# Splitting attention keys once and copying the other half by DMA, value weights' low parts on VectorE, roots one tile later

## The chip, the cores and the metric

The kernel runs on one core of one Trainium2 chip. A core has five engines, each with its own instruction queue: TensorE (PE in the profile, with its weight loads as PEld), VectorE (DVE), ScalarE (ACT), GpSimd (POOL) and the sync engine (SP), which issues all of this kernel's DMAs. Each queue is worked off in order; an instruction that waits holds back what stands behind it on its engine. Tensors lie on chip in 128 partitions. The metric is the device time of one launch in microseconds (us), as the median of several runs; one more launch was profiled.

## The reference, cut to what matters

The reference is two layers of a diffusion backbone over 512 latent tokens and 256 context tokens, 1024 wide, in float32. The change lies in layer 0, grouped-query attention with 16 query heads and 4 key and value heads of 64 elements:

```
q_l, k_l, v_l = split(h_lat @ w_qkv)
q_l = rope(rms_norm(q_l, q_norm));  k_l = rope(rms_norm(k_l, k_norm))
k_c, v_c likewise for the context, normed, without rope
s = einsum(q, k) * HEAD_DIM ** -0.5
o = einsum(softmax(s), v) @ w_o
```

Latent queries attend to all 768 keys, context queries to the 256 context keys. Behind it come a gated feed-forward layer with a short convolution, a Mamba-2 layer in both directions and a second feed-forward layer. All of these take most of the time and are not edited.

## The kernel before, in words

Activations are kept transposed: features on partitions, tokens in columns (512 latent, then 256 context). To keep float32 accuracy every operand of the large products is split into a high part, rounded to TensorE's reduced float32, and a low part, what the rounding left; a product then takes three matmuls: high by high, high by low and low by high (`mm3`, L105 to L108). `split` (L81) does this with a cast on ScalarE (L85) and a subtraction on VectorE or GpSimd (L87).

Attention starts with a stage written out by hand, in which PE multiplies the latent tokens by six column tiles of the query and key weights into `ps_l`. The loop that the change edits comes next (L694 to L705). For the same six tiles, in the order 0, 1, 2, 4, 5, 3, it multiplies the context tokens (24 matmuls into `ps_c`) and copies the result behind the latent columns of `raw0` to `raw5`. Tile 0 holds keys 0 and 1 (two heads of 64 elements, one on each half of the partitions), tile 1 the first two query heads, tile 3 keys 2 and 3, the others more queries.

Between the tiles stand steps of two generators, `keys(0, ...)` and `queries(0, ...)`. Both begin with `normed` (L526): squares (L529) and gain (L530) on ScalarE, a copy of the latent columns with neighbouring groups of 32 partitions swapped by four DMAs (`qsw`, L533), the rotary turn in three VectorE operations (L534 to L536), sums over each head by matmuls with two columns (`ssq`, L236), the inverse root (`rsa`, `rsy`, `rsu`, `rbq`, L239 to L247), a transposition of the root by PE (`rsTq`, L253, four and then two blocks of 128 tokens), and the multiplication by it (L540). `normed` yields after `rbq`, and after each of the two groups of transpositions. So the step in which PE transposes needs the `rbq` of the step before. `keys` then makes, for each of its two heads, a high and a low tile in which the head stands on both halves of the partitions (L547 to L555), since two query heads, one per half, are multiplied by the same key head; `queries` splits into `qh` and `ql`.

Also in this loop the two halves of the value weights are loaded and split (`wv`), the low parts on GpSimd (`wl`). When the loop is done, 48 steps of `values` (three matmuls each into `ps_v`, L521) are walked through; at every fifth a step of `pairs[0].maxima()` stands between them (L602: scores of the high parts only, whose row maxima on VectorE, L604, give the shift `diag` of the softmax), and at every sixth a step of the queries of pair 1. Then follow eight pairs of query heads with scores (`ps_s`, L674), exponentials (`pr`, L677) and products with the values (`ps_o`, L638); pair p uses key head p // 2. Keys 2 and 3 are made during these pairs (`keys(1, ...)`), with the rotary turn on GpSimd.

A scheduler sets the order behind the hand-written stage: it takes the instructions by the order in which the program wrote them and by a model of when each can start. Tiles of 128x768 come from a ring of 18 buffers (`t3`).

Of the kernel before, what the change touches and what calls it, by code (L numbers as in the profile page):

```python
# [9 lines left out]
F32R = mybir.dt.float32r  # L10
AF = mybir.ActivationFunctionType
ALU = mybir.AluOpType
# [55 lines left out]
def t3(g, name, dt=F32, n=T):  # L68
    return g.t3p.tile([P, n], dt, tag="t3", bufs=g.n3, name=name)
# [6 lines left out]
def _r(ap):  # L76

    return ap.bitcast(F32)


def split(g, src, hi, lo, lo_engine="dve", pin=False):  # L81

    nc = g.nc
    keep = g.tc.keep_in_program_order if pin else lambda i: i
    keep(nc.scalar.copy(hi, src))  # L85
    eng = nc.vector if lo_engine == "dve" else nc.gpsimd
    keep(eng.tensor_tensor(lo, src, _r(hi), ALU.subtract))  # L87


def load_w(g, dram, lo_engine="dve", pin=False):  # L90

    st = t4(g, "wst")
    wh = t4(g, "wh", F32R)
    wl = t4(g, "wl", F32R)
    g.nc.sync.dma_start(st, dram)
    split(g, st, wh, wl, lo_engine=lo_engine, pin=pin)
    return wh, wl
# [282 lines left out]
def attention(g, fill, X, late):  # L380


    nc, I = g.nc, g.I
    S64 = slice(0, 64), slice(64, 128)
# [62 lines left out]
    e = g.p.tile([P, 2 * KT], F32, name="silu")  # L447
# [8 lines left out]
    rsl, _, _ = next(norm)  # L456
# [12 lines left out]
    for m in range(KT):  # L469
# [14 lines left out]
        if m == 4:  # L484
            rsc = t3(g, "rsc", n=C)
            pt, _, _ = next(norm)
# [23 lines left out]
    wv = []  # L510
# [33 lines left out]

    def keys(j, qs, eng):
        yield from normed(qs, kn, eng)
        for e in range(2):  # L547

            h, l = t3(g, f"kh{j}{e}", F32R), t3(g, f"kl{j}{e}", F32R)
            s, o = S64[e], S64[1 - e]  # L550
            nc.scalar.copy(h[s], qs[s])
            nc.scalar.copy(h[o], qs[s])
            nc.vector.tensor_tensor(l[s], qs[s], _r(h)[s], ALU.subtract)
            nc.scalar.copy(l[o], _r(l)[s])
            k2[2 * j + e] = (h, l)  # L555
        yield 0

    qprep = {}
# [26 lines left out]
    class Pair:  # L585
# [6 lines left out]
        def maxima(self):  # L592


            qh, kh = qprep[self.p][0], k2[self.kv][0]
            lat, ctx, mz = small("ma"), small("mb"), small("mz")

            def scores(ts, k0, n, out):
                ps = Sb("ps_m")
                for i, t in enumerate(ts):  # L600
                    for e in range(2):
                        nc.tensor.matmul(ps[:, 512 * e + n * i : 512 * e + n * i + n], qh[S64[e], t * P : (t + 1) * P],  # L602
                                         kh[S64[e], k0 : k0 + n], start=True, stop=True)
                nc.vector.reduce_max(out[:, :, ts[0] : ts[-1] + 1], ps.rearrange("p (e t k) -> p e t k", e=2, k=n),  # L604
                                     axis=AX.X, negate=True)

            scores((4, 5), L, C, lat)
            nc.vector.tensor_copy(ctx[:, :, 4:], lat[:, :, 4:])
            yield
            for t in (0, 2):  # L610
                scores((t,), 0, L, lat)
                yield
                scores((t + 1,), 0, L, lat)
                yield
                scores((t, t + 1), L, C, ctx)
                if t:

                    for e in range(2):
                        for h in range(2):
                            nc.vector.tensor_tensor(mz.rearrange("p h t -> p t h")[S64[e], :, h], lat[S64[h], e],  # L620
                                                    ctx[S64[h], e], ALU.min)
                    self.diag = g.t3p.tile([P, T], F32R, tag="mrow", bufs=2, name=f"diag{self.p}")
                    v = self.diag.rearrange("p (t h q) -> p t h q", h=2, q=64)
                    for h in range(2):
                        nc.vector.tensor_tensor(v[:, :, h], id2.unsqueeze(1).broadcast_to([P, T // P, 64]),
                                                mz[:, h].unsqueeze(2).broadcast_to([P, T // P, 64]), ALU.mult)
                yield

        def steps(self):

            (qh, ql), (kh, kl) = qprep[self.p], k2[self.kv]
            po = acc = None
            o = g.t3p.tile([P, T], F32, tag="o", bufs=2, name=f"o{self.p}")

            def values(po, pr, t, off, n, first, last):
                v = vt[t][:, self.kv * HD : (self.kv + 1) * HD]
                for e in range(2):
                    nc.tensor.matmul(po[S64[e], :n], v, pr[:, 512 * e + off : 512 * e + off + n], start=first, stop=last)  # L638

            def final(po, ps, acc, out):  # L640

                n = out.shape[-1]
                for e in range(2):
                    nc.tensor.matmul(ps[S64[e], :n], g.ones[:, :HD], acc[:, n * e : n * e + n], start=True, stop=True)
                y, u = t2("y")[:, :n], t2("u")[:, :n]

                nc.scalar.activation(y, ps, AF.Ln)
                nc.scalar.activation(y, y, AF.Exp, scale=-1.0)
                nc.vector.tensor_tensor(out, po, y, ALU.mult)
                nc.vector.scalar_tensor_tensor(u, ps, -1.0, y, ALU.mult, ALU.mult)  # L650
                nc.vector.scalar_tensor_tensor(out, u, 2.0, out, ALU.add, ALU.mult)

            def later_lat(po, pr, t, acc):
                values(po, pr, t, 0, L, t == 0, t == 5)
                if t == 5:
                    final(po, Bk("ps_sum"), acc, o[:, :L])

            def later_ctx(pr, acc):
                pc = Bk("ps_oc")
                for t in range(2):  # L660
                    values(pc, pr, 4 + t, C * t, C, t == 0, t == 1)
                final(pc[:, :C], pc[:, C:], acc, o[:, L:])
                if self.p < 6:
                    nc.sync.dma_start(odram[self.p], o)

            prev = None
            for t in range(7):
                ps, pr = Sb("ps_s"), g.t3p.tile([P, 1024], F32, tag="pr", bufs=3, name="pr")
                for q0, n, k0, off in (((0, L, t * P, 0),) if t < 6 else ((L, C, L, 0), (L, C, L + P, C))):
                    q, k = slice(q0, q0 + n), slice(k0, k0 + P)  # L670
                    outs = [ps[:, 512 * e + off : 512 * e + off + n] for e in range(2)]
                    for i, (a, b) in enumerate(((kh, qh), (kl, qh), (kh, ql))):
                        for e in range(2):
                            nc.tensor.matmul(outs[e], a[S64[e], k], b[S64[e], q], start=i == 0, stop=False)  # L674
                    for e in range(2):
                        nc.tensor.matmul(outs[e], onesr[S64[e]], self.diag[S64[e], q], start=False, stop=True)  # L676
                nc.scalar.activation(pr, ps, AF.Exp)  # L677
                if t == 0:
                    po = Bk("ps_o")
                elif t == 1:  # L680
                    acc = g.t3p.tile([P, 1024], F32, tag="acc", bufs=1, name="acc")
                    nc.vector.tensor_tensor(acc, prev, pr, ALU.add)
                elif t < 6:
                    nc.vector.tensor_tensor(acc, acc, pr, ALU.add)
                else:
                    acc = t2("accc")
                    halves = pr.rearrange("p (e k q) -> p e k q", e=2, k=2)
                    nc.vector.tensor_tensor(acc.rearrange("p (e q) -> p e q", e=2), halves[:, :, 0], halves[:, :, 1], ALU.add)
                prev = pr
                yield (lambda t=t, pr=pr, po=po, acc=acc: later_lat(po, pr, t, acc)) if t < 6 else (  # L690
                    lambda pr=pr, acc=acc: later_ctx(pr, acc))
            g.o.append(o)

    early = []  # L694
    for n, j in enumerate((0, 1, 2, 4, 5, 3)):
        ps = Bk("ps_c")
        for k in range(KT):
            k_step(k, j, ps[:, :C], hc)
        nc.scalar.copy(raw[j][:, L:], ps[:, :C])
        if n in (1, 3):  # L700
            wv.append(load_w(g, I["wv"][len(wv)], lo_engine="pool", pin=True))
        if n in (1, 2):
            early.append(keys(0, raw[0], nc.vector) if n == 1 else queries(0, raw[1], nc.vector))
        for gen in early:
            next(gen, None)  # L705
    vals = values()
    for gen in early:
        for _ in gen:
# [22 lines left out]

    m = pairs[0].maxima()
    for i, _ in enumerate(vals):
        if i % 5 == 0:
            next(m, None)
        if i % 6 == 5:
            next(qgen[1], None)
# [706 lines left out]
```

## Time and profile before

| what | value |
|---|---|
| timed runs | 1899.8, 1905.27, 1905.67 us; median 1905.27 us |
| profiled execution, its own time | 1901.6 us |
| its span, first to last instruction | 1899.8 us |
| TensorE busy | 1864.1 us, 98% |
| VectorE busy | 1313.6 us, 69% |
| ScalarE busy | 820.2 us, 43% |
| GpSimd busy | 308.8 us, 16% |
| mean granted TensorE clock | 0.994 |

The span leaves out 1.8 us that lie around it. A busy PE is not a PE at its peak, since matmuls overlap and their ends are modelled; what counts here is where PE has no matmul under way, and what ended that idle time, which a row of the timeline shows in brackets behind the instruction. In the edited stretch, from 63 to 112 us, every step hangs on PE's order: an instruction of PE that waits holds back all matmuls behind it.

### The profile page before, as it was taken

The page shows a single profiled execution, that of the slowest core. Times are in us where ns is not written, and L with a number is a line of the kernel's source. Part 1 is how long each engine was busy: PE and PEld are TensorE (multiplying, and loading weights), DVE is VectorE, ACT ScalarE, POOL GpSimd, SP SyncE. Part 2 cuts the span into 40 slices and gives each one's busy share as a digit, 9 for nine tenths or more (in the row PEclk, how much of TensorE's full clock was granted, in tenths as well). Part 3 has the DMA queues.
Part 4 walks back from the last instruction along what each step waited for, and adds up shares of the span by engine and source line. Part 5 has one row for each costly group of instructions (what it writes and reads, how often), then busy time and mean ns, then how long its engine had stood idle before and what let it go on. Part 6 is the DMA issues. An engine that isn't in the chain of part 4 may idle for free.

```text
span 1899.8 us, 28697 instructions
## 1 busy us (share of the span) xinstructions
PE 1864.1 (98%) x11426; PEld 1548.5 (82%) x11426; DVE 1313.6 (69%) x1949; ACT 820.2 (43%) x1420; POOL 308.8 (16%) x268
## 2 busy tenths in 40 slices
PE   9899999999999999999999999999999999999999
PEld 7775564688888888888888888888887878888887
DVE  6578778678777776444487877777788466565555
ACT  4635344254222222222266676776666352323331
POOL 2241111040000000000041334444333210000000
PEclk9999999999999999999999999999999999999999
DMA  9221341014433553122223334434453223323232
GB/s 340 84 84 45 115 142 67 34 50 176 153 123 120 190 188 135 67 67 67 67 86 115 118 89 122 123 113 132 122 153 107 85 78 97 98 83 111 89 100 89
DMA packets 73430, 210.10 MB, mean 111 GB/s; under 512 B 8912, under 2 KB 14416, under 8 KB 73168
## 3 DMA queue, kind: packets, MB, share of 16 engines
q1 hardware_dynamic: 73296, 208.26, 33.7%
q8 instruction: 90, 1.47, 0.3%
q14 instruction: 44, 0.36, 0.1%
HBM read 198.79 MB, written 6.82 MB: 108 GB/s over the span
## 4 chain that ended last, share of the span: by engine, by line
PE 79%; DVE 10%; issue 4%; ACT 2%; DMA 2%; POOL 1%; SPq 0%; POOLq 0%; DVEq 0%; ACTq 0%
PE ps_up L106 10%; PE ps_up L108 10%; PE ps_up L105 10%; PE ps_d L105 6%; PE ps_d L106 6%; PE ps_d L108 6%; PE ps_in L108 4%; PE ps_in L106 4%; PE ps_in L105 4%; PE ps_o L638 2%; PE ps_s L674 2%; PE ps_st L1034 2%; DVE ht L281 1%; PE ps_wo L108 1%; PE ps_wo L105 1%
## 5 line engine op out<-in xcount | busy, mean ns | idle before, releaser
L87 DVE TENSOR_TENSOR wl<-wst,wh 128x1024 fp32r<-128x1024 f32 x205 | 258.1, 1259 | 238.7 <-PE ps_up L106 128.2
L85 ACT CAST wh<-wst 128x1024 fp32r<-128x1024 f32 x211 | 221.2, 1049 | 407.3 <-DMA wst<-in_wup 330.3
L106 PE MATMUL ps_up<-hlf,wh 128*128 128x512 f32 (+1 forms) x1008 | 357.0, 354 | 0.0
L108 PE MATMUL ps_up<-hhf,wl 128*128 128x512 f32 (+1 forms) x1008 | 356.8, 354 | 0.0
L105 PE MATMUL ps_up<-hhf,wh 128*128 128x512 f32 x1008 | 356.8, 354 | 0.0
L106 PEld LDWEIGHTS ps_up<-hlf,wh 128*128 128x128 f32 x1008 | 190.6, 189 | 26.4
L105 PEld LDWEIGHTS ps_up<-hhf,wh 128*128 128x128 f32 x1008 | 190.5, 189 | 26.5
L108 PEld LDWEIGHTS ps_up<-hhf,wl 128*128 128x128 f32 x1008 | 190.5, 189 | 26.3
L105 PE MATMUL ps_in<-hhs,wh 128*128 128x512 f32 (+1 forms) x560 | 204.4, 365 | 1.2 <-ACT dt L919 1.2
L106 PE MATMUL ps_in<-hls,wh 128*128 128x512 f32 (+1 forms) x560 | 199.3, 356 | 0.0
L108 PE MATMUL ps_in<-hhs,wl 128*128 128x512 f32 (+1 forms) x560 | 198.7, 355 | 0.0
L105 PE MATMUL ps_d<-hdh,wh 128*128 128x512 f32 (+1 forms) x568 | 193.4, 342 | 0.2 <-ACT hdh L85 0.2
L108 PE MATMUL ps_d<-hdh,wl 128*128 128x512 f32 (+1 forms) x568 | 193.5, 341 | 0.0
L106 PE MATMUL ps_d<-hdl,wh 128*128 128x512 f32 (+1 forms) x568 | 192.9, 340 | 0.3 <-DVE hdl L87 0.3
L785 DVE SCALAR_TENSOR_TENSOR X<-ps_d,mod,X 128x512 f32<-128x512 f32 (+1 forms) x224 | 124.3, 583 | 35.0 <-PE ps_d L108 34.8
L105 PEld LDWEIGHTS ps_in<-hhs,wh 128*128 128x128 f32 x560 | 105.9, 189 | 16.4 <-ACT dt L919 1.4
L106 PEld LDWEIGHTS ps_d<-hdl,wh 128*128 128x128 f32 x568 | 106.7, 188 | 14.8 <-DVE hdl L87 0.7
L108 PEld LDWEIGHTS ps_in<-hhs,wl 128*128 128x128 f32 x560 | 105.8, 189 | 14.7
L108 PEld LDWEIGHTS ps_d<-hdh,wl 128*128 128x128 f32 x568 | 106.7, 188 | 13.1
L105 PEld LDWEIGHTS ps_d<-hdh,wh 128*128 128x128 f32 x568 | 106.3, 188 | 13.6 <-ACT hdh L85 0.7
L106 PEld LDWEIGHTS ps_in<-hls,wh 128*128 128x128 f32 x560 | 106.0, 189 | 13.2
L677 ACT ACTIVATE pr<-ps_s 128x1024 f32<-128x1024 f32 x56 | 57.2, 1022 | 107.1 <-PE ps_s L676 106.2
(338 smaller groups left out, 3536.8 us busy)
## 6 DMA issues: line engine op xcount, KB each, us to landing
wst<-in_wup SPq DMA_DIRECT2D x88, 512.0 KB, 3.3
wada<-in_adaT SPq DMA_DIRECT2D x56, 512.0 KB, 3.4
wst<-in_win SPq DMA_DIRECT2D x48, 512.0 KB, 3.5
wst<-in_wdown SPq DMA_DIRECT2D x44, 512.0 KB, 3.7
E<-ad SPq DMA_DIRECT2D x64, 256.0 KB, 6.5
wada<-in_adaB SPq DMA_DIRECT2D x24, 512.0 KB, 4.2
ec<-ead SPq DMA_DIRECT2D x64, 128.0 KB, 5.2
wst<-in_wout SPq DMA_DIRECT2D x16, 512.0 KB, 3.4
```

Of the source, the lines that this page charges most:

```text
L85: keep(nc.scalar.copy(hi, src))
L87: keep(eng.tensor_tensor(lo, src, _r(hi), ALU.subtract))
L105: mm(out, wh, ah, start=first, stop=False)
L106: mm(out, wh, al, start=False, stop=False)
L108: mm(out, wl, ah, start=False, stop=last)
L281: nc.vector.scalar_tensor_tensor(t[:, c0:c1], ap, g.moda[layer][ca][:, m, v : v + 1], rs[:, c0:c1], ALU.mult, ALU.mult)
L638: nc.tensor.matmul(po[S64[e], :n], v, pr[:, 512 * e + off : 512 * e + off + n], start=first, stop=last)
L674: nc.tensor.matmul(outs[e], a[S64[e], k], b[S64[e], q], start=i == 0, stop=False)
L677: nc.scalar.activation(pr, ps, AF.Exp)
L785: nc.vector.scalar_tensor_tensor(ap, o[:, c0:c1], gate[:, m, v : v + 1], ap, ALU.mult, ALU.add)
L1034: nc.tensor.matmul(ps[:, d * 256 : (d + 1) * 256], Bt[:, t * P : (t + 1) * P], xw[d][t], start=t == ts[0], stop=t == ts[-1])
```

## The change

Four things change, all in `attention`.

1. `keys` splits the two heads of a tile at once, on all 128 partitions, into a high and a low tile (`kh`, `kl`). Four DMAs then write a second pair (`khs`, `kls`) with the halves exchanged. Each head now finds its high part for one half of the partitions in the one tile and for the other half in the other; the scores and the maxima pick the tile by half. Before, four casts, two subtractions and two copies on half the partitions made four such tiles.
2. The value weights' low parts are computed on VectorE instead of GpSimd.
3. The steps of the first keys and queries stand at other tiles: behind tile n = 1 the keys' sums and root, behind 2 the queries', behind 3 both groups of the keys' transpositions, behind 4 both of the queries' and then the keys' split, behind 5 the queries' split. Before, the keys' first group stood behind 2, and the queries' behind 3.
4. The maxima of pair 0 stand at the value steps 2, 7, 12 and so on instead of 0, 5, 10.

```diff
     def keys(j, qs, eng):
         yield from normed(qs, kn, eng)
-        for e in range(2):
-
-            h, l = t3(g, f"kh{j}{e}", F32R), t3(g, f"kl{j}{e}", F32R)
-            s, o = S64[e], S64[1 - e]
-            nc.scalar.copy(h[s], qs[s])
-            nc.scalar.copy(h[o], qs[s])
-            nc.vector.tensor_tensor(l[s], qs[s], _r(h)[s], ALU.subtract)
-            nc.scalar.copy(l[o], _r(l)[s])
-            k2[2 * j + e] = (h, l)
+        nat = t3(g, f"kh{j}", F32R), t3(g, f"kl{j}", F32R)
+        swp = t3(g, f"khs{j}", F32R), t3(g, f"kls{j}", F32R)
+        split(g, qs, *nat)
+        for a, b in zip(swp, nat):
+            for e in range(2):
+                nc.sync.dma_start(_r(a)[S64[e]], _r(b)[S64[1 - e]])
+        k2[2 * j], k2[2 * j + 1] = (nat, swp), (swp, nat)
         yield 0
...
-            qh, kh = qprep[self.p][0], k2[self.kv][0]
+            qh, kh = qprep[self.p][0], [h for h, _ in k2[self.kv]]
...
-                                         kh[S64[e], k0 : k0 + n], start=True, stop=True)
+                                         kh[e][S64[e], k0 : k0 + n], start=True, stop=True)
...
-                    for i, (a, b) in enumerate(((kh, qh), (kl, qh), (kh, ql))):
+                    for i, (a, b) in enumerate(((0, qh), (1, qh), (0, ql))):
                         for e in range(2):
-                            nc.tensor.matmul(outs[e], a[S64[e], k], b[S64[e], q], start=i == 0, stop=False)
+                            nc.tensor.matmul(outs[e], kk[e][a][S64[e], k], b[S64[e], q], start=i == 0, stop=False)
...
-    early = []
+    early = [keys(0, raw[0], nc.vector), queries(0, raw[1], nc.vector)]
...
         if n in (1, 3):
-            wv.append(load_w(g, I["wv"][len(wv)], lo_engine="pool", pin=True))
-        if n in (1, 2):
-            early.append(keys(0, raw[0], nc.vector) if n == 1 else queries(0, raw[1], nc.vector))
-        for gen in early:
-            next(gen, None)
+            wv.append(load_w(g, I["wv"][len(wv)], pin=True))
+        for i in {1: "k", 2: "q", 3: "kk", 4: "qqk", 5: "q"}.get(n, ""):
+            next(early[i == "q"])
...
-        if i % 5 == 0:
+        if i % 5 == 2:
             next(m, None)
```

How the instructions stand on PE, behind the context tiles n = 2 and n = 3 (two pieces of the difference; `ps_c` is a context tile, `ssq` the sums of the queries' squares, `rsTq` a transposed root):

```order
 L108 MATMUL ps_c<-hha_7_132,wsl 128x256
-L253 MATMUL rsTq<-cst,rbq 128x128 x4
 L236 MATMUL ssq<-cst,qsq 128x2 x6
 L105 MATMUL ps_c<-hha_0_118,wsh 128x256
...
 L108 MATMUL ps_c<-hha_7_132,wsl 128x256
-L253 MATMUL rsTq<-cst,rbq 128x128 x2
+L253 MATMUL rsTq<-cst,rbq 128x128 x6
 L105 MATMUL ps_c<-hha_0_118,wsh 128x256
```

The four transpositions of the keys' root that stood behind tile n = 2 now stand with the other two behind n = 3; those of the queries' root move in the same way from behind n = 3 to behind n = 4.

VectorE from the end of the keys' rotary turn on (`raw_898` is the keys' tile, `raw_899` the queries'):

```order
+L247 SCALAR_TENSOR_TENSOR rbq<-rsu,rsy 128x768
 L540 TENSOR_TENSOR raw_898<-raw_898,rsTq 128x512
-L247 SCALAR_TENSOR_TENSOR rbq<-rsu,rsy 128x768
 L540 TENSOR_TENSOR raw_898<-raw_898,rsTq 128x256
+L87 TENSOR_TENSOR wl<-wst,wh 128x1024
+L87 TENSOR_TENSOR kl_1140<-raw_898,kh_1139 128x768
 L534 TENSOR_TENSOR raw_899<-raw_899,cs 128x512
 L535 TENSOR_TENSOR qsw<-qsw,cs 128x512
-L553 TENSOR_TENSOR kl_1136<-raw_898,kh_1135 64x768
+L540 TENSOR_TENSOR raw_899<-raw_899,rsTq 128x256
 L536 TENSOR_TENSOR raw_899<-raw_899,qsw 128x512
```

The queries' root is now made ahead of the keys' multiplication, and the second value weight's low part and the keys' low part stand ahead of the queries' rotary turn.

SP's queue behind the queries' swap (`wada` and `wst` are weights, `raw_900` and `raw_902` the queries of pairs 1 and 2):

```order
 L533 DMA qsw<-raw_899 32x512 x4
-L122 DMA wada<-in_adaB 128x1024 x4
-L95 DMA wst<-in_wq 128x1024
+L122 DMA wada<-in_adaB 128x1024
+L552 DMA khs_1141<-kh_1139 64x768 x2
+L552 DMA kls_1142<-kl_1140 64x768 x2
+L122 DMA wada<-in_adaB 128x1024
 L533 DMA qsw<-raw_900 32x512 x4
+L122 DMA wada<-in_adaB 128x1024 x2
+L95 DMA wst<-in_wq 128x1024
 L533 DMA qsw<-raw_902 32x512 x4
```

The four copies stand behind one weight load, and three weight loads and a query weight that stood ahead of pair 1's swap now stand around and behind it.

More of the change, by code (lines that the diff above doesn't have):

```diff
@@ L629, in steps @@
         def steps(self):
-            (qh, ql), (kh, kl) = qprep[self.p], k2[self.kv]
+            (qh, ql), kk = qprep[self.p], k2[self.kv]
             po = acc = None
```

## The prediction

> **What bounds the kernel now.** I read the page first: who is busy, and the chain that ended last.
>
> ```profile
> span 1899.8 us, 28697 instructions
> PE 1864.1 (98%) x11426; PEld 1548.5 (82%) x11426; DVE 1313.6 (69%) x1949; ACT 820.2 (43%) x1420; POOL 308.8 (16%) x268
> PE 79%; DVE 10%; issue 4%; ACT 2%; DMA 2%; POOL 1%; SPq 0%; POOLq 0%; DVEq 0%; ACTq 0%
> ```
>
> TensorE (PE) sets the end; all its idle time is 1899.8 - 1864.1 = 35.7 us. The change edits a short stretch, so next I read the windows there: PE's busy time comes first after the length, the granted clock stands after POOL.
>
> ```profile
> 70.00:80.00 10.00, 8.58 (x74) 8.15 (x73) 6.49 (x12) 4.23 (x10) 2.40 (x1) 1.00 0.66 191
> 80.00:90.00 10.00, 8.03 (x67) 7.72 (x68) 8.99 (x11) 8.27 (x12) 2.71 (x1) 1.00 0.52 178
> 90.00:100.00 10.00, 10.00 (x80) 8.97 (x79) 6.19 (x10) 2.69 (x6) 3.84 (x3) 1.00 0.13 29
> 220.00:480.00 260.00, 252.35 (x1732) 183.03 (x1731) 201.60 (x326) 112.70 (x182) 32.26 (x31) 0.99 0.26 89
> ```
>
> Between 70 and 90 us PE idles 20 - 8.58 - 8.03 = 3.39 us; after it PE is full again, and 97% busy up to 480 us, so time won here should reach the end. PE's waits and its timeline name the idle pieces:
>
> ```profile
> PE rsTq L253 <- DVE rbq L247: 2.1, 2, 1.2
> PE ps_m L602 <- ACT qh L85: 1.3, 1, 1.3
> PE ssq L236 <- ACT qsq L529: 0.9, 1, 0.9
> ...
> 74.81 0.66 PE L253 MATMUL rsTq<-cst,rbq 128*128 128x128 f32 x4 [1.18 <-DVE rbq L247]
> 75.30 1.40 PE L236 MATMUL ssq<-cst,qsq 128*128 128x2 f32 x12
> 79.39 0.38 PE L253 MATMUL rsTq<-cst,rbq 128*128 128x128 f32 x2
> 80.70 0.63 PE L253 MATMUL rsTq<-cst,rbq 128*128 128x128 f32 x4 [0.93 <-DVE rbq L247]
> 88.76 0.50 PE L602 MATMUL ps_m<-kh,qh 64*128 64x256 f32 x4 [1.27 <-ACT qh L85]
> 93.11 1.88 PE ps_v L521 x15
> ```
>
> Keys' roots 1.18, queries' roots 0.93, the first maxima 1.27: 3.38 us, all of the idle time. (The last row is from the chain: value matmuls follow each other every 1.88 / 15 = 0.125 us.) Why the roots are late stands in DVE's and POOL's timelines:
>
> ```profile
> 71.04 2.40 POOL L87 TENSOR_TENSOR wl<-wst,wh 128x1024 fp32r<-128x1024 f32 x1 [5.61 <-issue]
> 71.52 1.95 DVE L243 TENSOR_TENSOR rsu<-rsy,rsa 128x12 f32<-128x12 f32 x1 [0.52 <-ACT rsy L241]
> 73.79 0.96 DVE L247 SCALAR_TENSOR_TENSOR rbq<-rsu,rsy 128x768 f32<-128x768 f32 x1
> 77.55 0.69 DVE L535 TENSOR_TENSOR qsw<-qsw,cs 128x512 f32<-128x512 f32 x1
> 78.15 0.16 DVE L243 TENSOR_TENSOR rsu<-rsy,rsa 128x12 f32<-128x12 f32 x1
> 79.60 0.95 DVE L247 SCALAR_TENSOR_TENSOR rbq<-rsu,rsy 128x768 f32<-128x768 f32 x1
> 81.03 2.71 POOL L87 TENSOR_TENSOR wl<-wst,wh 128x1024 fp32r<-128x1024 f32 x1 [7.59 <-ACT wh L85]
> 81.40 2.89 DVE L535 TENSOR_TENSOR qsw<-qsw,cs 128x512 f32<-128x512 f32 x1
> ```
>
> While POOL subtracts a value weight's low part, a DVE instruction that takes 0.16 us elsewhere takes 1.95, and one of 0.69 takes 2.89; both end when POOL does. The locks cost DVE 1.79 and 2.20 us, just ahead of what PE waits for.
>
> **The change, part by part.** *Later roots.* PE stood ready for the keys' transposes at 74.81 - 1.18 = 73.6. Now it goes on: row sums of the queries (1.4) to 75.0, a context tile (from 76.6 to 79.39 above, so 2.8) to 77.8, six transposes (0.8: issued in 0.5 and 0.3, ahead of the ends shown) to 78.6, a tile to 81.4, six transposes to 82.2, the last tile to 85.0, nine value matmuls to 86.1, and there the first maxima stand. Before, they ran at 88.76 behind three value matmuls; six more at 0.125 make that 89.5. Without a new wait that is 3.4 us.
>
> *Is everything there in time?* DVE does its first low part (1.26, first row below) where the lock cost 1.79, so the keys' root is ready by 74.75 as before; needed at 77.8. The queries' took 79.60 + 0.95 - 76.6 = 3.9 us behind its sums, so 78.9 now; needed at 81.4. Both covers exceed 2 us. The keys are multiplied by 79.5 (0.69 + 0.41 behind 78.4). Then come low part two and the keys' own low part (0.96) to 81.8, the queries' five operations at starts some 0.6 apart to 84.6, and qh (0.83) at 85.5. Needed at 86.1: cover 0.6 us. This is the tightest compute cover; what is late behind it is PE itself.
>
> ```profile
> L87 DVE TENSOR_TENSOR wl<-wst,wh 128x1024 fp32r<-128x1024 f32 x205 | 258.1, 1259 | 238.7 <-PE ps_up L106 128.2
> L551 ACT CAST kh<-raw x2: 839/840/842, 80.9 to 82.6; 64x768 fp32r<-64x768 f32 x2
> L553 DVE TENSOR_TENSOR kl<-raw,kh x2: 941/948/955, 84.2 to 85.8; 64x768 fp32r<-64x768 f32 x2
> 85.19 0.83 ACT L554 CAST kl<-kl 64x768 fp32r<-64x768 f32 x1 [0.59 <-DVE kl L553]
> 87.88 0.83 ACT L85 CAST qh<-raw 128x768 fp32r<-128x768 f32 x1 [0.21 <-DVE raw L540]
> 88.74 0.96 DVE L87 TENSOR_TENSOR ql<-raw,qh 128x768 fp32r<-128x768 f32 x1 [0.94 <-ACT qh L85]
> ```
>
> *Keys split once.* ACT loses four casts and two copies of 0.83 or 0.84 (5.0 us) and gains one cast of qh's shape (0.83); DVE loses two subtractions of 0.95 and gains one of 0.96. Around 180 us the same happens to keys 1. I cost the shorter ACT and DVE work itself at nothing: PE is full there, and for keys 0 it only lengthens the covers above.
>
> *The copies.* Four DMAs of 64x768 (192 KB each) per key pair are new. Their nearest rows are the rotary swaps, 64 KB each:
>
> ```profile
> L533 SPq DMA_DIRECT2D qsw<-raw x24: 507/582/1079, 69.1 to 128.1; - x24
> DMA to landing us min/median/max: 1.9/2.2/4.9
> ```
>
> kh is ready at 80.4; two issues of 0.58 put the second high copy out by 81.5, so it lands between 83.4 and 86.4. Needed at 86.2: a stall of 0 to 0.2 us. I take 0, since the median lands at 83.7. Three times the bytes could add 2 to 4 us; a landing of 6.5 would stall PE 1.8, the upper bound. [...] Behind the copies on SP's queue stand ada weights, pair 1's rotary swap and a query weight, whose DMAs wait if kh or kl does. Both are ready by 81.8, and the swap's input is only made behind qh, after 85.5, so that costs nothing. The low copies are first read with the scores, over 20 us later. In the second key pair the copies wait at about 180 us, four pairs before use.
>
> *What is late next.* DVE now has pair 1's L540 ahead of the fourth maxima reduction. L540 waits for POOL's rotary work, whose input is made some 3 us sooner, as PE arrives sooner. If POOL is late, PE misses a bank by at most about one such operation: 0 to 0.7, taken 0. Starting the maxima two steps later leaves `diag` ample cover:
>
> ```profile
> 107.74 1.03 DVE L625 TENSOR_TENSOR diag<-id,mz 128x384 fp32r<-128x384 f32 x2
> 111.94 0.50 PE L674 MATMUL ps_s<-qh,kh 64*128 64x512 f32 x2
> 112.50 2.36 POOL L87 TENSOR_TENSOR wl<-wst,wh 128x1024 fp32r<-128x1024 f32 x1
> 114.90 1.05 ACT L85 CAST wh<-wst 128x1024 fp32r<-128x1024 f32 x1 [0.70 <-POOL wl L87]
> 117.08 2.72 PE L236 MATMUL ssq<-cst,qsq 128*128 128x2 f32 x12 [0.94 <-ACT qsq L529]
> 116.00:120.00 4.00, 3.06 (x16) 2.90 (x16) 3.60 (x4) 2.73 (x5) 2.35 (x1) 0.60 0.13 39
> 120.00:124.00 4.00, 4.00 (x56) 2.25 (x58) 3.15 (x6) 2.10 (x4) 0.00 (x0) 0.54 0.37 110
> ```
>
> *The first scores.* PE waits 0.94 us for qsq behind a weight cast that waited for POOL. The first query weight's cast and low part now come earlier, so POOL no longer holds the second cast; its DMA does, some 0.5 us sooner relative to the scores. I take -0.5 (bounds -0.9 and 0).
>
> **Sum.** -3.4 - 0.5 = -3.9 us; the profiled execution's span becomes 1895.9 and its own time 1901.6 - 3.9 = 1897.7. The timed runs had 1899.8, 1905.27 and 1905.67; their median, 3.7 above the profiled time, would become 1901.4. Between the two I forecast 1900.
>
> **The rivals.**
>
> *The clock falls less.* In the last two rows the granted clock is 0.60 and 0.54: (0.40 + 0.46) x 4 = 3.4 us of clock lost behind a stretch of idle time and tiny row sums. The stretch at 73.6 to 76.7 looks alike (1.18 idle, 0.5, 1.4) and kept clock 1.00 here; in the runs 4 us slower it may not have. The change fills the one and shortens the other. If that saves the 3.4 us: -7.3, or 1898 from the median. Against: some sums remain, and the fall may simply move. [...]
>
> *The gain is given back.* Later pairs wait for ACT, DVE or DMAs at times that do not move, and the 3.9 us are lost among PE's 260 - 252.35 = 7.6 idle us up to 480: no change, 1905. Against it: these waits hang on PE's own results and on buffers that PE frees.
>
> *Slower.* The high copies land late, 6.5 us after issue. PE then idles 1.8 us at one place, right behind nine matmuls, and the clock falls as at 116 us, costing 3.4: -3.9 + 1.8 + 3.4 = +1.3, or 1906.6; it decides from a landing past 4.7 us with a fall of both windows. For it speaks the slowest swap, 4.9; against it, an idle DMA at that time.
>
> *The change does not do what it says*, if the order of instructions kept the waits; the transposes stand a tile later, so I give it nothing apart.
>
> **How the numbers follow.** Forecast 0.50, clock 0.25, given back 0.16, slower 0.09. For one measurement 0.3%, 5.7 us, is about what can be told from no change. The forecast lies at 0.2%; run scatter (1899.8 to 1905.67) puts a quarter of it past 0.3%, the clock case mostly: 0.13 + 0.23 = 0.36 faster. Of the slower case 0.06 exceeds 0.3%; 0.58 the same. The range takes in the clock case with some scatter and the given-back case: 1893.5 to 1905.5. The forecast's own is 1896 to 1904.
>
> **What would show it.** Right: no PE wait for `rbq` before 90 us; the first ps_m some 2.6 us earlier, unwaited; DVE's L535 at 0.69 twice; the first ps_s near 108.5 instead of 111.94; the ssq wait below 0.94. Wrong: a PE wait on `khs` or qh there, POOL still at wl before 90 us, DVE's reduction late near 100 us, or a first ps_s that is early while the span is not.

## The result, and the profile after

The changed kernel takes 1896.49 us (median of 8 runs, 1892.56 to 1899.04) against 1900.87 us of the kernel before (8 runs, 1898.9 to 1905.67). The ratio is 0.9969, 95% interval [0.9958, 0.9981]: 5.9 us less, with 3.6 to 8.0 as its ends. The forecast was 1900 us with 3.9 us less; the time lies inside its range, and the gain is larger than its sum. Eight runs of the kernel before have a median of 1900.87 us where the first three had 1905.27, so the gain, and not the time, is what to compare.

The head of the page of the kernel after:

```profile
span 1894.8 us, 28684 instructions
PE 1864.3 (98%) x11426; PEld 1549.6 (82%) x11426; DVE 1315.9 (69%) x1949; ACT 811.8 (43%) x1410; POOL 302.6 (16%) x266
```

The span is 5.0 us shorter and PE's busy time is the same (1864.1 before): what went is idle time. The same windows as before the change (PE's busy time first, the granted clock behind POOL) and PE's waits from 60 to 200 us:

```profile
70.00:80.00 10.00, 10.00 (x90) 10.00 (x89) 6.29 (x13) 5.34 (x12) 0.00 (x0) 1.00 0.39 107
80.00:90.00 10.00, 10.00 (x89) 9.73 (x87) 7.67 (x13) 4.38 (x7) 0.00 (x0) 1.00 0.66 191
220.00:480.00 260.00, 252.82 (x1725) 183.95 (x1725) 203.36 (x329) 113.69 (x182) 31.97 (x31) 0.99 0.26 91
...
PE ps_s L672 <- ACT pr L675: 1.8, 1, 1.8
PE ps_l L105 <- ACT hha L290: 1.1, 1, 1.1
PE ps_m L600 <- DVE ma L602: 1.1, 2, 0.6
```

PE is full from 70 to 90 us, where it had idled 3.39 us, and up to 200 us no wait for `rbq`, qh or ssq is left. The wait for hha (the high part of the normed tokens) stands at 60 us, ahead of all edited code. The waits for ma (a row maximum, at 119.5 and 133.3 us) and for pr (an exponential, at 197.4 us) are not new. The kernel before has them too, in these rows of its timeline:

```profile
136.55 0.50 PE L602 MATMUL ps_m<-kh,qh 64*128 64x512 f32 x2 [1.19 <-DVE ma L604]
200.57 0.39 PE L674 MATMUL ps_s<-qh,kh 64*128 64x256 f32 x2 [1.66 <-ACT pr L677]
```

With the wait for ssq (0.94) that makes 3.8 us between 110 and 230 us before, and 0.43 + 0.63 + 1.79 = 2.85 us after. The timelines of PE, DVE and ACT in the edited stretch, after:

```profile
74.69 1.39 PE L236 MATMUL ssq<-cst,qsq 128*128 128x2 f32 x12
78.86 0.82 PE L253 MATMUL rsTq<-cst,rbq 128*128 128x128 f32 x6
82.25 0.82 PE L253 MATMUL rsTq<-cst,rbq 128*128 128x128 f32 x6
86.81 0.38 PE L600 MATMUL ps_m<-kh,qh 64*128 64x256 f32 x1
...
73.32 0.16 DVE L243 TENSOR_TENSOR rsu<-rsy,rsa 128x12 f32<-128x12 f32 x1
76.94 0.69 DVE L535 TENSOR_TENSOR qsw<-qsw,cs 128x512 f32<-128x512 f32 x1
83.03 0.69 DVE L535 TENSOR_TENSOR qsw<-qsw,cs 128x512 f32<-128x512 f32 x1
85.49 0.83 ACT L85 CAST qh<-raw 128x768 fp32r<-128x768 f32 x1 [2.66 <-DVE raw L540]
```

All of it stands some 1.2 us later than it would with the prologue (the code ahead of 60 us) of the first profile, which had no such wait for hha. A second profile of the changed kernel has no such wait either, and its first context matmul starts at 63.54 us against 63.74 before the change, so its times compare when 0.2 us is taken off the gain:

```profile
85.38 0.38 PE L600 MATMUL ps_m<-kh,qh 64*128 64x256 f32 x1
107.78 0.49 PE L672 MATMUL ps_s<-qh,kh 64*128 64x512 f32 x1
```

The first maxima stand at 85.38 instead of 88.76, and the first scores at 107.78 instead of 111.94. Less the 0.2 us, 4.0 us are won by the first scores, where the forecast had 3.4.

### The profile page after: what moved, and what is told of

Its sections match the earlier page's. It is cut to its first block, busy times and chain, and to the rows that moved or that the text cites. A ratio compares the mean times of both kernels' runs of the same rounds, so it can differ in the third digit from the quotient of the medians.

```text
span 1894.8 us, 28684 instructions
## 1 busy us (share of the span) xinstructions
PE 1864.3 (98%) x11426; PEld 1549.6 (82%) x11426; DVE 1315.9 (69%) x1949; ACT 811.8 (43%) x1410; POOL 302.6 (16%) x266
## 4 chain that ended last, share of the span: by engine, by line
PE 82%; DVE 10%; issue 4%; ACT 2%; POOL 1%; DMA 1%; POOLq 0%; SPq 0%; DVEq 0%; ACTq 0%
PE ps_up L106 10%; PE ps_up L108 10%; PE ps_up L105 10%; PE ps_d L105 6%; PE ps_d L106 6%; PE ps_d L108 6%; PE ps_in L108 4%; PE ps_in L106 4%; PE ps_in L105 4%; PE ps_s L672 2%; PE ps_o L636 2%; PE ps_st L1030 2%; DVE ht L281 1%; PE ps_wo L108 1%; PE ps_wo L105 1%
```

## How the runs were split into two parts

The runs of one kernel scatter by 8 us and more, which is above the effect. Each lists its span and mean granted clock, so the clock lost is (1 - clock) x span, and the rest of its time is what it would take at full clock. The clock is listed to 0.001, 1.9 us of a run, so only means are of use. The two parts need not be independent: what PE waits for can arrive while it runs at half speed. Each ratio is against the kernel before on the same chip (medians 1903.08, 1901.92 and 1902.64 us in three sets; for the change's first ratio the 1900.87 above). The two means are over all runs of a kernel that list a clock, with standard errors, the change's and the unshifted kernel's over both of their sets. The eight runs behind 1900.87 list none, so the change's first set is compared here with other sets of the kernel before.

```
kernel                           runs  median   ratio [95%]              at full clock  clock lost
before                            76   -        1                        1891.6 +-0.2   11.4 +-0.4
the change                        13   -        0.9969 and 0.9966        1888.3 +-0.6    7.9 +-0.8
roots alone (e1)                  10   1896.61  0.9961 [0.9949, 0.9974]  1888.1 +-0.3    8.9 +-0.9
low parts on VectorE alone (e2)   12   1902.67  0.9994 [0.9981, 1.0006]  1891.1 +-0.5   10.9 +-0.8
keys split once alone (e3)        11   1900.48  0.9982 [0.9971, 0.9992]  1890.4 +-0.3   10.0 +-0.7
change, maxima unshifted          14   -        0.9951 and 0.9965        1887.0 +-0.5    8.4 +-0.9
change, low parts on POOL (e8)     8   1897.58  0.9974 [0.9965, 0.9984]  1888.9 +-1.0    8.3 +-0.9
change, query lows on DVE (e6)    10   1897.14  0.9969 [0.9960, 0.9979]  1887.5 +-0.5    9.3 +-0.4
before, waits filled (e11)        12   1905.45  1.0004 [0.9991, 1.0018]  1894.4 +-0.4   10.3 +-0.8
change, split deferred (e9)       12   1899.69  0.9987 [0.9976, 0.9998]  1892.9 +-0.2    7.1 +-0.8
e9, maxima unshifted (e10)        12   1900.57  0.9990 [0.9978, 1.0002]  1892.4 +-0.3    7.8 +-0.6
```

## The experiments: one part of the change at a time

**Roots alone (e1).** The kernel before with the order of `early` and the start of the maxima as in the change:

```
-    early = []
+    early = [keys(0, raw[0], nc.vector), queries(0, raw[1], nc.vector)]
...
+        for i in {1: "k", 2: "q", 3: "kk", 4: "qqk", 5: "q"}.get(n, ""):
+            next(early[i == "q"])
...
-        if i % 5 == 0:
+        if i % 5 == 2:
```

> The kernel before with the roots alone one context tile later (and the maxima two value steps later); the value weights' low parts stay on POOL and the keys are split as before. Theory of the forecast (POOL's subtraction locks DVE and the lock counts): PE's two waits for rbq, 1.18 and 0.93 us, vanish; DVE's L243 and L535 still take about 2 and 2.9 us beside POOL, so the queries reach qh 1.5 to 3 us later than in the change and the first ps_m waits 1 to 2.5 us; net -0.5 to -2.4 us on the time before, taken -1.5. Rival (the covers swallow the locks, order is all): no wait of the first ps_m, -3.4 us, as much as the whole change.

PE's waits from 60 to 110 us and DVE's operations beside POOL, of this kernel:

```profile
PE ps_m L602 <- ACT qh L85: 0.4, 1, 0.4
...
72.14 1.96 DVE L243 TENSOR_TENSOR rsu<-rsy,rsa 128x12 f32<-128x12 f32 x1 [0.52 <-ACT rsy L241]
80.44 2.87 DVE L535 TENSOR_TENSOR qsw<-qsw,cs 128x512 f32<-128x512 f32 x1
```

The locks are as long as before (1.96 and 2.87 us), and still only 0.4 us of the waits is left, not 1 to 2.5. The order alone gives as much as the whole change, 0.9961 against 0.9969 and 0.9966. The rival is right up to this 0.4 us, and the expectation from the locks is refuted.

**Low parts on VectorE alone (e2).** `load_w(..., lo_engine="pool", pin=True)` becomes `load_w(..., pin=True)` in the kernel before.

> The kernel before with the two value weights' low parts on VectorE alone. Theory of the forecast: L243 takes 0.16 and L535 0.69 us everywhere ahead of 90 us; the low part costs 1.26 where the locks cost 1.79 and 2.20, so the first wait for rbq shrinks from 1.18 to about 0.65, the second from 0.93 to about 0, the first ps_m's from 1.27 to under 0.8; sum -2 us. Rival (the locks lie beside slack): PE's waits stay, no change.

PE's waits, and DVE and POOL where the new one lies:

```profile
PE rsTq L253 <- DVE rbq L247: 1.7, 1, 1.7
PE ps_m L602 <- ACT qh L85: 1.0, 1, 1.0
...
95.65 1.98 DVE L247 SCALAR_TENSOR_TENSOR rbq<-rsu,rsy 128x768 f32<-128x768 f32 x1
...
96.89 1.86 POOL L536 TENSOR_TENSOR raw<-raw,qsw 128x512 f32<-128x512 f32 x1
```

Both early waits for `rbq` are gone, more than expected. But pair 1's root, 0.96 us elsewhere, now falls beside POOL's rotary work, takes 1.98, and PE waits 1.70 for it. With 1.02 left at the first maxima that is 2.7 us of waits up to 100 us where the first profile before had 3.4: a gain of 0.7 here, and 0.5 +- 0.5 at full clock over the runs. The 2 us expected are not won. That the edit brought the new wait about isn't shown: the second profile of the unchanged kernel (below) has the same wait, 1.72 us, at the same instruction.

**Keys split once alone (e3).** Only `keys` and its readers as in the change:

```
+        split(g, qs, *nat)
+        for a, b in zip(swp, nat):
+            for e in range(2):
+                nc.sync.dma_start(_r(a)[S64[e]], _r(b)[S64[1 - e]])
```

> The kernel before with only the keys split once on all partitions and copied by transfers. Theory of the forecast: ACT loses 5.0 us and DVE 1.9 us per key pair at keys 0 off the path; the first ps_m still waits for qh by 1 to 1.3 us since qh waits for DVE and not for ACT; nothing waits for khs; 0 to -0.3 us. Rival (ACT's six keys' operations are what makes qh late): the wait of 1.27 us vanishes and -1.3 us is won. Slower rival: khs lands more than 4.7 us behind its issue and PE waits for it, +1 us or more.

```profile
75.09 0.66 PE L253 MATMUL rsTq<-cst,rbq 128*128 128x128 f32 x4 [1.18 <-DVE rbq L247]
80.98 0.63 PE L253 MATMUL rsTq<-cst,rbq 128*128 128x128 f32 x4 [0.93 <-DVE rbq L247]
87.97 0.38 PE L600 MATMUL ps_m<-kh,qh 64*128 64x256 f32 x1 [0.22 <-ACT qh L85]
```

The roots' waits stay as they were, and that for qh falls from 1.27 to 0.22: the shorter chain of key work ahead of qh counts, and 1.2 +- 0.4 us is won at full clock. The first rival is right here. Nothing waits for `khs`. At full clock the three parts alone give 3.5, 0.5 and 1.2 us, 5.2 together, and the change 3.4: they fill the same waits.

**Low parts back on POOL (e8).** The change with `lo_engine="pool"` for the value weights, which leaves roots and key split.

> The change with the value weights' low parts back on POOL (roots one tile later and keys split once stay). Theory of the forecast (the locks count): L243 1.95 and L535 about 2.9 us again, the queries' chain ends up to 1.5 us later, qh at 87.3 instead of 86.3 where PE is ready at 86.8: the first ps_m waits 0.5 to 1 us, so part two of the change is worth that much. Rival (covers swallow it): no wait of the first ps_m, part two is worth nothing once the roots are later.

```profile
80.58 2.88 DVE L535 TENSOR_TENSOR qsw<-qsw,cs 128x512 f32<-128x512 f32 x1
...
86.82 0.38 PE L600 MATMUL ps_m<-kh,qh 64*128 64x256 f32 x1 [0.39 <-ACT qh L85]
```

DVE is locked for 2.2 us, and PE waits 0.39, so the rest falls into the covers. Part two is worth 0.4 us of idle time here, less than the 0.5 to 1 expected and not nothing; the runs can't show it (0.9974 against 0.9966). Beside e1, whose wait is 0.41, it also shows that the key split adds next to nothing once the roots are later.

**The cover of qh (e4).** The change with `i % 5 == 0` again, so that the first maxima stand behind one value step.

> The change with the first pair's maxima back behind one value step instead of three, 0.75 us sooner. Theory of the forecast (qh has 0.5 us of cover in the change, khs 1.7): the first ps_m waits 0.2 to 0.6 us for qh and not for khs; the span is that of the change within 0.6 us, 1895 to 1895.5, if the clock falls as there. Rival (any new wait there makes the clock fall again): one more stretch at half speed ahead of 100 us, 1.7 to 3.4 us more. Second rival: the two steps are worth what they move, 0.75 us.

The first maxima wait 0.23 us for qh (0.22 in a second profile), as expected, and not for `khs`, and the clock falls nowhere between 66 and 108 us, so the first rival is wrong. The ratio of 0.9951 [0.9936, 0.9967] leaves open whether the shift costs time. The same kernel again:

> The change with the maxima where they were, a second time. Theory (its first result, 1.3 us below the change's median of another chip, is scatter): the ratio to the kernel before is within 0.0010 of the change's 0.9966. Rival (the two value steps cost time): a ratio of 0.995 again, 1 to 3 us below the change.

The second ratio is 0.9965 [0.9952, 0.9977]: the same as the change. The two value steps are worth nothing that these runs can show.

## The experiments: the clock

**The change again, and the kernel before again.**

> The change itself once more, on the chip and beside the runs of the kernel before that the next kernels have. The time of a run is taken as two parts, the time at full clock and the clock lost, (1 - mean granted clock) x span. Theory (idle time alone): the part at full clock is 3.4 to 3.9 us below the kernel before, the clock lost the same as before (within 1 us). Rival (the clock falls less, the forecast's second case): the same 3.4 to 3.9 us, and the mean clock lost is 2 to 3.4 us less as well, -6 to -7.3 us in all.

The ratio is 0.9966 [0.9953, 0.9978], 6.5 us. Over its two sets the change has 3.4 us less at full clock (standard error 0.6), and 3.5 us less clock lost (0.9); in this set alone it is 2.1 (1.0) and 4.6 (1.2). The rival is right as to the amount; how it divides is known no better than these errors.

> The kernel before, profiled a second time. Theory (the clock is granted in windows of 3.41 us that run on their own, and a stretch with little work brings one or two of them to half speed by where it lies in a window): idle times and waits between 66 and 136 us as in the first profile within 0.2 us, but half-speed stretches at other places or in other number, each 3.4 or 6.8 us long and all starts a multiple of 3.41 us apart. Rival (a given stretch of the program brings the clock down each time): the same four stretches as in the first profile, at the same places of the program.

The second profile of the kernel before, 1906.84 us: PE's timeline, and the windows at its half-speed stretches up to 108 us.

```profile
76.08 0.66 PE L253 MATMUL rsTq<-cst,rbq 128*128 128x128 f32 x4 [1.18 <-DVE rbq L247]
76.58 1.40 PE L236 MATMUL ssq<-cst,qsq 128*128 128x2 f32 x12
90.99 0.50 PE L602 MATMUL ps_m<-kh,qh 64*128 64x256 f32 x4 [1.67 <-ACT qh L85]
101.97 0.91 PE L253 MATMUL rsTq<-cst,rbq 128*128 128x128 f32 x4 [1.72 <-DVE rbq L247]
...
76.00:80.00 4.00, 3.92 (x28) 3.92 (x29) 1.98 (x6) 0.43 (x2) 0.00 (x0) 0.79 0.65 196
80.00:84.00 4.00, 4.00 (x29) 3.96 (x29) 3.13 (x7) 1.52 (x3) 0.07 (x1) 0.78 0.89 310
92.00:96.00 4.00, 4.00 (x22) 3.34 (x20) 1.93 (x3) 1.86 (x2) 0.00 (x0) 0.57 0.22 51
100.00:104.00 4.00, 2.28 (x14) 2.07 (x12) 3.05 (x2) 0.00 (x0) 2.97 (x2) 0.78 0.00 0
104.00:108.00 4.00, 4.00 (x26) 3.17 (x25) 2.15 (x3) 1.04 (x2) 0.00 (x0) 0.79 0.00 0
```

The program's waits are not quite the same: the keys' wait is again 1.18, qh's is 1.67, and pair 1's root costs 1.72 as in e2, which it did not in the first profile. Behind each of these three the clock falls to half for 3.4 us: (0.21 + 0.22) x 8 from 78.3 on, 0.43 x 8 in the second, 0.43 x 8 from 102.2 on. The first profile had none of these three falls. The spacing in the theory holds: the third begins 23.9 us behind the first, 7.0 times 3.41 (the 3.413 us of the clock records below), and the rival's four stretches at the same places do not come back. That waits stay within 0.2 us does not hold. So the stretch that the prediction named (1.18 idle, 0.5, 1.4) does lose its clock in some executions and keep it in others. That this hangs on where it lies in a window is the author's guess; no run tests it.

The half-speed stretches of the changed kernel's first profile, by its windows:

```profile
120.00:124.00 4.00, 3.87 (x23) 2.79 (x24) 3.90 (x8) 2.59 (x4) 0.00 (x0) 0.77 0.70 233
124.00:128.00 4.00, 4.00 (x16) 1.71 (x14) 3.44 (x5) 1.34 (x3) 3.31 (x3) 0.50 0.72 211
128.00:132.00 4.00, 4.00 (x23) 2.31 (x24) 4.00 (x4) 2.04 (x2) 4.00 (x3) 0.87 0.24 94
284.00:288.00 4.00, 2.65 (x10) 1.10 (x10) 4.00 (x5) 0.17 (x1) 1.04 (x1) 0.75 0.31 123
288.00:292.00 4.00, 4.00 (x16) 1.79 (x14) 3.73 (x5) 1.02 (x1) 0.00 (x0) 0.50 0.02 4
```

At half speed, 0.23 x 8 = 1.84 us of the first window are slow, so the stretch begins at 122.16; the other begins at 286.00 by the same working. The trace's own clock records have both at 0.50 for 6.827 us, from 122.189 and from 286.029, and one more for 3.413 us from 1525.067. Between the first two lie 163.84 us, 48.0 times 3.413. In the first profile of the kernel before, the records have four between 60 and 1898 us, of 6.827, 3.413, 6.827 and 3.413 us, from 116.823, 202.156, 290.903 and 1529.941 on: the last three begin 25.0, 51.0 and 414.0 times 3.413 us behind the first. In all profiles a stretch lasts 3.4 us or a multiple, unless the end of the trace cuts it short, and costs 1.7 us of clock for each 3.4. Measured from the kernel's start, the stretches at 116.8 and 78.3 us of the two profiles of the kernel before lie 11.3 windows apart, not a whole number.

**The waits filled with work (e11).** The kernel before, with matmuls of ones ahead of the waiting instructions, in the two transposes and the first maxima:

```
         pt = bank(f"rsT{name}")
+        for _ in range(g.filler.pop(0) if name == "q" and g.filler else 0):
+            nc.tensor.matmul(pt[:, :P], g.ones, g.ones, start=True, stop=True)
...
                 ps = Sb("ps_m")
+                for _ in range(g.filler.pop(0) if g.filler else 0):
+                    nc.tensor.matmul(ps[:, :P], g.ones, g.ones, start=True, stop=True)
...
+    g.filler = [4, 0, 3, 0, 4]
```

> The kernel before with matmuls of ones put into its three waits: four ahead of the keys' transposes, three ahead of the queries', four ahead of the first maxima, into the bank that the waiting instructions overwrite. Each is two records of 0.138 us (10 of them in 1.38 us at the start of the trace), so they fill 1.1, 0.83 and 1.1 us of the waits of 1.18, 0.93 and 1.27. The work arrives no sooner. Theory (idle stretches bring the clock down, and that is the part of the change's gain which the forecast left out): the part of the time at full clock stays within 0.7 us of the kernel before, the mean clock lost is 2 to 4 us less, so 2 to 4 us faster without any wait removed. Rival (the tiny row sums bring it down, or the clock's share of the gain is chance): clock lost and time as before, or +0.3.

PE's timeline with the fillers, and its waits from 60 to 140 us:

```profile
73.64 1.05 PE L253 MATMUL rsTq<-ones 128*128 128x128 f32 x8
...
PE ssq L236 <- ACT qsq L531: 2.1, 1, 2.1
PE ps_m L606 <- ACT qh L85: 0.7, 1, 0.7
```

The fillers stand where they should (the second group takes 0.83 us), and no time is won: 1.0004 [0.9991, 1.0018]. The clock lost is 10.3 +- 0.8 us, 1.1 less than in the kernel before and not clearly different from it, and the time at full clock is 2.8 +- 0.5 us more, where the theory allowed 0.7. So the theory in this form falls. As a test of idle time it is weak, for two reasons. In the first profile of the kernel before, none of the three filled waits had a fall behind it, and between 66 and 108 us its second one lost three windows, 5.1 us. And the fourth wait, that of ssq at 116 us, was not filled; it is 2.10 us here against 0.94, and a row of three half-speed windows begins within it.

The traces say more on what precedes a fall. These are the 3.41 us ahead of one in e3, and those of the fall:

```profile
113.21:116.62 3.41, 3.27 (x28) 2.70 (x27) 2.76 (x4) 3.38 (x6) 3.04 (x3) 1.00 0.51 154
116.63:120.04 3.41, 3.41 (x16) 1.79 (x19) 3.34 (x6) 1.29 (x4) 0.65 (x1) 0.50 0.43 149
```

PE idles only 0.14 us there, but 1.92 us of the window are row sums with two columns. In e1, ahead of its fall at 114.6 us, it is 0.20 us of idle time and 1.86 us of row sums. The second profile of the kernel before has the opposite ahead of 102.2 us, 1.72 us of idle time and no row sum. So idle time isn't needed for a fall, and row sums aren't either. How much of either it takes is not shown: in the unshifted kernel's second profile a window with 0.14 and 1.62 us had no fall behind it.

The eleven kernels also show an association: those with the roots later lose 7.1 to 9.3 us of clock on average, those with the roots where they were 10.0 to 11.4. The half-speed windows of their profiles, nine of the former and five of the latter, say where, counted per profile: from 66 to 108 us none against 0.8, from 108 to 220 us 1.3 against 3.2, and from 220 us to the end 2.2 against 1.8. Most of the difference lies behind the edited stretch, in the first scores and the pairs behind them, and it is there that a cause would have to be sought.

## The experiments: two attempts at more

**Query weights' low parts on VectorE (e6).** In `queries`, `load_w(g, I["wq"][p - 4])` without the POOL engine.

> The change with the four query weights' low parts on VectorE too, so that POOL computes no weight's low part in attention. Theory (POOL's subtraction locks DVE, and in the change the two locks between 111 and 118 us are what PE waits for at 119.5 and 133.3): L606, L243 and L244 take 0.17 each there instead of 1.58, 1.31 and 2.28, PE's two waits for ma, 1.1 us in all, vanish; -1.1 us against the change, 1895.3 against 1896.4 if the clock is the same. Rival (DVE, busy 23.2 of 24 us there, pays for the subtractions itself, 2 x 1.26 us): the waits for ma stay or grow, 0 to +1.5 us.

PE's timeline of this kernel:

```profile
113.64 0.50 PE L672 MATMUL ps_s<-qh,kh 64*128 64x512 f32 x1 [0.89 <-ACT pr L675]
131.46 0.49 PE L600 MATMUL ps_m<-kh,qh 64*128 64x512 f32 x1 [1.63 <-DVE ma L602]
```

DVE's small operations between 111 and 118 us are short again (0.16, 0.16 and 0.17), and yet PE waits 1.63 for ma, and 0.89 for pr. 0.9969 [0.9960, 0.9979], the change's ratio. The rival is right as to the time. The wait of 0.43 at 119.5 us is gone, as the theory had it, but not the other. The rival's reason for that is not shown: DVE's two subtractions end by 113 us, 17 us ahead of the wait for ma, and a wait for ma of 0.6 to 1.8 us stands between 128 and 144 us in every profile of this study, before the change too. Since the locks are gone and it stays, the theory had the wrong cause for it; the right one stays open.

**The split deferred (e9, e10).** PE's 1.8 us wait for pr (1.66 in the kernel before) stands behind a cast that waits 3.4 us for its weight's transfer:

```
-            w = load_w(g, I["wq"][p - 4], lo_engine="pool")
+            st, w = t4(g, "wst"), (t4(g, "wh", F32R), t4(g, "wl", F32R))
+            nc.sync.dma_start(st, I["wq"][p - 4])
+            yield BREAK
+            split(g, st, *w, lo_engine="pool")
```

> The change with the query weights' split one break of their generator behind their transfer, so that ScalarE's cast does not stand in front of the exponentials while its transfer is still out. Theory (in the change PE waits 1.8 us near 197 us for pr behind a cast that waits 3.4 us for its transfer, and the clock falls there in several profiles): that wait vanishes, -1.8 us of idle time and up to -1.7 us of clock; 1892 to 1894 us. Rival (later steps of the generators then come too late for the next pair, or the wait moves): 0 to +3 us against the change.

PE's waits from 60 to 480 us in e9:

```profile
PE ps_m L603 <- DVE ma L605: 3.2, 4, 1.7
PE ps_m L603 <- ACT qh L85: 2.6, 4, 1.2
PE rsTq L253 <- DVE o L650: 1.7, 1, 1.7
```

The wait for pr is gone, and those for ma (1.1 us in the change), qh (0.5) and a root (0.4) have grown by 5.5 us together against the change's first profile, and by 2.9 us against its second (2.4, 0.5 and 1.7). It is 4.6 us more at full clock than the change. The rival is right; that the queries of the next pairs now come late fits the waits for qh and was not tested by itself.

> The last kernel with the first maxima behind one value step as before the change. Theory (the 0.75 us by which the maxima move sooner cost only the 0.2 us wait for qh and make no work, so the shift itself is worth nothing at the end): within 0.6 us of the last kernel. Rival (the earlier maxima let the first scores' stretch start with more cover): another 1 to 1.5 us faster.

0.9990 [0.9978, 1.0002], as e9: the shift is worth nothing here either. No kernel of this study is shown to beat the change.

## Why the prediction was right, and where not

- **The idle time (-3.4): right.** No wait for `rbq`, the first maxima unwaited, PE full from 70 to 90 us. From the same start the first maxima come 3.2 us earlier (forecast 2.6) and the first scores 4.0 (forecast 3.4), 0.6 more than counted. An estimate for that is the restart behind a wait. In a running row a context matmul takes 0.28 us and starts 0.12 behind the one ahead, so the two overlap by 0.16; behind a wait there is nothing to overlap with. Three waits make 0.5 us.
- **What makes the roots late: half right.** The locks were read rightly and vanish (0.16, 0.69), and in e2, without them, so do both waits for the roots. (The second locked instruction ended 0.55 us behind POOL's, 84.29 against 83.74, and not with it.) But e1 and e8 show that a tile of cover swallows all but 0.4 us of the locks; the order alone is enough.
- **The covers: right.** qh ends at 85.49 + 0.83 = 86.32, 0.5 us ahead of its use (forecast 0.6); without the shift PE waits 0.23. The high copies land well ahead, by this answer on `khs` from 78 to 90 us in the change's first profile:

```profile
L552 SPq DMA_DIRECT2D khs<-kh x2: 510/549/588, 81.4 to 82.0; - x2
DMA to landing us min/median/max: 2.7/2.9/3.1
```

  The last is there by 85.1, 1.7 us early. Their median is 2.9 us, 0.7 above the 2.2 of the swaps in the kernel before, for three times the bytes, where the prediction's estimate was 2 to 4 us more. The slower rival asked for more than 4.7 us and fell. What the prediction held against it, an idle DMA, was misread: its own row from 80 to 90 us has a DMA share of 0.52. The copies were in time at 0.66 after the change.
- **The key split at nothing: right in the sum, wrong in its reason.** Alone it wins about 1 us of PE's wait for qh, which the prediction missed: it took the shorter chain for cover only. Behind later roots it is worth next to nothing (0.41 us of wait in e1 without it, 0.39 in e8 with it), so the sum was not touched.
- **What is late next: right.** DVE's L540 of pair 1 stands ahead of the fourth reduction, and PE does not wait there.
- **The first scores (-0.5): right in size.** The ssq wait of 0.94 is gone. Of the other waits from 110 to 230 us, those for ma and pr, the kernel before has 2.85 us, the change 2.85 in its first profile and 3.40 in its second, so 0.9 and 0.4 us are won there. Two profiles are few, and the waits move by as much between executions: the kernel before has 4.5 us of all these waits in its second profile and 3.8 in its first. POOL's subtractions lock DVE for longer after the change (1.58, 1.31 and 2.28 us between 111 and 118 us, where one instruction took 2.07 before), which the step did not name.
- **The clock, left out of the sum: this is the step that failed.** The prediction made it a rival, all or nothing, at 3.4 us, and kept it out because the fall might simply move; in the first profile after, it did move, from 117 to 122 us. Over the runs the mean clock lost falls by 3.5 us +- 0.9, and the time at full clock by 3.4 +- 0.6. Together that is some 6.8 us in the means, nearer to the rival's 7.3 (chance 0.25) than to the forecast's 3.9 (chance 0.50); the two ratios say 5.9 and 6.5. One profile could not show it: what the clock costs is a mean over executions. Why it falls less stays open.
- **The time: partly by the width of the range.** The forecast of 1900 lies between two bases, and the range of 12 us holds the case of no change too. That 1896.49 lies inside says little; the waits that went say more.
- **The gain given back: no.** From 220 to 480 us PE is busy 252.82 of 260 us, against 252.35.

## What to carry to other kernels

When a result stands late, ask first whether the instructions that wait can stand later: here the order alone gave the whole gain. With that cover in place, taking the low parts off GpSimd was worth 0.4 us of PE's waiting, and the key split next to nothing. Before a wait is put down to a change, look for it in the kernel before, in more than one profile: the waits for ma and pr, and that for pair 1's root, were there already. For effects below 0.5%, split each run into its time at full clock and the clock that it lost before reading a profile's clock as the kernel's.

## What the runs showed of the hardware that was not expected

In these profiles the clock falls to 0.50 for 3.41 us or a multiple, at places that differ from one execution to the next. From 60 us on, the stretch that the end of the trace cuts short left out, a profile loses between 1 and 8 such windows (1.7 to 14 us), and a fall needs no long wait of PE ahead of it: 1.18 us of waiting beside transposes and row sums is followed by one in one execution and not in another, and in e3 one follows 0.14 us of waiting beside 1.92 us of row sums. GpSimd's and VectorE's operations took longer beside each other, both ways: the third rotary operation took POOL 1.29 us at its first two places in the kernel before, and 1.86 beside DVE's root in e2, which itself took 1.98 instead of 0.96.
